# A macaron layer on one core: gate/up and down of each SwiGLU as one woven sequence, the sum of eight pairs scaled once, engines issuing in the written order

## The chip, the cores and the metric

The kernel runs on one core of one Trainium2 chip. The metric is the device time of one execution in microseconds. A core has five engines with an instruction queue each: PE multiplies matrices, ACT (ScalarE), DVE (VectorE) and POOL (GpSimd) work on tiles of 128 partitions, and SP issues the DMA transfers here. Each queue is worked off strictly in its order; semaphores make an instruction wait for another engine or a transfer, and whatever stands behind it in its queue then waits too.

## The reference, cut to what matters

One layer with 1024 tokens, 1024 features and a hidden width of 2816, all in float32. The first and the last sub-layer, both a SwiGLU with half weight, are what the change touches; the token mixers and the attention to the memory lie between.

```python
def rmsnorm(x, g):
    xf = x.astype(jnp.float32)
    y = xf * lax.rsqrt(jnp.mean(xf * xf, axis=-1, keepdims=True) + EPS)
    return (y * g.astype(jnp.float32)).astype(x.dtype)

def swiglu(h, w_gu, w_down):
    gu = h @ w_gu
    gate, up = jnp.split(gu, 2, axis=-1)
    return (jax.nn.silu(gate) * up) @ w_down
...
x = x + 0.5 * swiglu(rmsnorm(x, ffn1_norm[l]), ffn1_w_gu[l], ffn1_w_down[l])
...
x = x + mixed @ w_out[l]
x = x + memory_cross_attention(rmsnorm(x, mem_q_norm[l]), rmsnorm(mem, mem_kv_norm[l]),
                               mem_w_q[l], mem_w_kv[l], mem_w_o[l])
x = x + 0.5 * swiglu(rmsnorm(x, ffn2_norm[l]), ffn2_w_gu[l], ffn2_w_down[l])
return rmsnorm(x, final_norm)
```

## The kernel before

**Tiles.** Activations lie with features on the partitions: 8 chunks of 128 features, each for two halves of H = 512 tokens (`xT[c, hf]`, tiles `x`). The normalised chunks are kept as a rounded part and a rest (`hh`, `hl`), and every float32 product is made of three matmuls of such parts (high by high, high by low, low by high; lines L258 to L260). The inverse RMS of a token is not in the activations: it is a row `rs` by which the gate and the up sums are multiplied later.

**Strassen's scheme.** The SwiGLU products are done by a scheme with seven products for a 2x2 block product (`PRODUCTS`): A11·B11, S1·T1, S2·T2, A12·B21, S3·T3, S4·B22, A22·T4. Their sums build up in the PSUM banks X, Y and Z (two buffers of each). A `job` is one such set for 256 columns of a weight matrix: it loads the weight (tiles `r`), POOL makes the sums S (L235 S1, L238 S2, L241 S4, L244 S3), and `blocks.factor` splits each factor into `f` (high part on ACT, L342; rest on DVE, L343). A product is jn x 3 matmuls of 128x512, with jn = 4 in gate and up. After a product its bank is read while later products run, and a bank is reused by another product about three products later.

**One SwiGLU.** The 2816 hidden features are 11 pairs of chunks. For each pair there is a gate job and an up job. `weave` lays the seven products of the jobs of two streams one beside the other, the second stream LAG = 3 products behind, and `prepare` makes the factors AHEAD = 6 products early. The reads (`summed`): L615 (ACT copies X or Y to a tile E), L622 (DVE adds a bank), L632 (times `rs`, on POOL, or on DVE for one block of four), L598 and L599 (`gated`: Silu on ACT, then a second multiplication by `rs` on POOL), L643 (DVE, up times gate). `store` (L689 to L694) forms T1 to T4 of the pair and sends seven tiles to DRAM.

**Down.** When gate and up are done, a second `weave` multiplies by the down weight: feature pairs in the groups (0,4), (4,4), (8,3), each with four jobs e = 0 to 3 of two output chunks. The last group of the second SwiGLU has two pairs, and the eleventh pair is multiplied plainly at the end. `staged` brings the stored tiles back into four landing buffers `sg` (L717), ACT copies the high part (L719), DVE makes the rest (L720). `fetch` (L729) brings x back from DRAM, and each bank is then added by DVE as x += 0.5·bank (L754, seven times per job and group).

**Ends.** At the start of a SwiGLU `sums` makes the T tiles of the input (L561 to L578). After its last group, ACT squares each finished chunk (`arrive`, L160), POOL adds the squares into `sqa` (L162), PE sums them over the partitions (tile `nm`, L187), and the chunks are lifted for the mixers (`lift_chunk`, L172 on ACT, L173 on DVE). A generator (`side`) normalises the memory rows between the pairs of the first SwiGLU.

**What sets the order.** The kernel names the engine of every instruction; the place in the engine's queue is chosen by the tile scheduler, within what the data allow.

## Time and profile before

| | us |
|---|---|
| three runs | 2341.6, 2348.91, 2348.41 (median 2348.41) |
| the profiled execution | 2342.71 |
| its span, first to last instruction | 2340.7 |
| DVE busy | 1602.7 (68%) |
| ACT busy | 980.3 (42%) |
| POOL busy | 765.0 (33%) |

The first SwiGLU fills about 0 to 700 us of the span, the second about 1667 us to the end. The profile's page lists the busy time of each engine; the table by stretches of time lists for each stretch the busy time of PE, PE's weight loads (PEld), DVE, ACT and POOL with the number of instructions, then the granted clock of PE (1.00 is full), the mean busy share of the 16 DMA engines and the GB/s moved. A busy PE may be a slow PE: the number of matmuls in a stretch says more than its busy time.

### The profile page before, as it was taken

The page shows a single profiled execution, that of the slowest core. Times are in us where ns is not written, and L with a number is a line of the kernel's source. Part 1 is how long each engine was busy: PE and PEld are TensorE (multiplying, and loading weights), DVE is VectorE, ACT ScalarE, POOL GpSimd, SP SyncE. Part 2 cuts the span into 40 slices and gives each one's busy share as a digit, 9 for nine tenths or more (in the row PEclk, how much of TensorE's full clock was granted, in tenths as well). Part 3 has the DMA queues.
Part 4 walks back from the last instruction along what each step waited for, and adds up shares of the span by engine and source line. Part 5 has one row for each costly group of instructions (what it writes and reads, how often), then busy time and mean ns, then how long its engine had stood idle before and what let it go on. Part 6 is the DMA issues. An engine that isn't in the chain of part 4 may idle for free.

```text
span 2340.7 us, 31188 instructions
## 1 busy us (share of the span) xinstructions
PE 2232.2 (95%) x11314; PEld 1869.8 (80%) x11314; DVE 1602.7 (68%) x2768; ACT 980.3 (42%) x1791; POOL 765.0 (33%) x720
## 2 busy tenths in 40 slices
PE   8899999889999999999999999999979999989998
PEld 6788878777878788887978888887768888877787
DVE  6755665768774878878697546567755555586777
ACT  6433443435454635345364333234533333343444
POOL 3555555522240202011022020001356565642223
PEclk9999999999999999999999999999989999999999
DMA  6232343465331000000014411111333333255432
GB/s 221 89 110 95 130 135 110 144 215 178 120 121 38 28 28 28 28 28 28 19 46 147 124 37 54 46 37 46 124 99 110 114 103 117 91 175 191 143 104 81
DMA packets 197529, 226.98 MB, mean 97 GB/s; under 512 B 10688, under 2 KB 139776, under 8 KB 197376
## 3 DMA queue, kind: packets, MB, share of 16 engines
q1 hardware_dynamic: 197376, 225.00, 29.7%
q8 instruction: 89, 1.46, 0.3%
q14 instruction: 64, 0.52, 0.1%
HBM read 165.45 MB, written 59.51 MB: 96 GB/s over the span
## 4 chain that ended last, share of the span: by engine, by line
PE 75%; DVE 12%; ACT 4%; issue 4%; POOL 3%; DMA 2%; SPq 0%; ACTq 0%; DVEq 0%; POOLq 0%
PE X L258 8%; PE X L259 8%; PE X L260 8%; PE acc L115 4%; PE acc L117 4%; PE acc L116 4%; PE Y L258 4%; PE Y L259 4%; PE Y L260 4%; DVE om L925 2%; PE Z L260 2%; PE Z L259 2%; PE Z L258 2%; PE q L115 2%; PE q L116 2%
## 5 line engine op out<-in xcount | busy, mean ns | idle before, releaser
L343 DVE TENSOR_TENSOR f<-S,f 128x512 fp32r<-128x512 f32 (+2 forms) x256 | 211.9, 830 | 175.6 <-ACT f L342 162.5
L342 ACT ACTIVATE f<-S 128x512 fp32r<-128x512 f32 (+2 forms) x256 | 155.1, 608 | 217.4 <-PE X L260 90.7
L258 PE MATMUL X<-T,f 128*128 128x512 f32 x488 | 196.3, 402 | 38.9 <-ACT E L615 15.4
L343 DVE TENSOR_TENSOR f<-r,f 128x512 fp32r<-128x512 f32 (+2 forms) x208 | 172.7, 833 | 65.8 <-ACT f L342 65.6
L258 PE MATMUL X<-hh,f 128*128 128x512 f32 x488 | 191.4, 392 | 14.2 <-DVE x L754 6.6
L259 PE MATMUL X<-T,f 128*128 128x512 f32 x488 | 195.0, 399 | 0.0
L260 PE MATMUL X<-T,f 128*128 128x512 f32 x488 | 194.8, 399 | 0.0
L342 ACT ACTIVATE f<-r 128x512 fp32r<-128x512 f32 (+2 forms) x208 | 125.6, 610 | 159.1 <-PE X L260 90.1
L259 PE MATMUL X<-hl,f 128*128 128x512 f32 x488 | 190.1, 389 | 0.0
L260 PE MATMUL X<-hh,f 128*128 128x512 f32 x488 | 190.0, 389 | 0.0
L235 POOL TENSOR_TENSOR S<-r,r 128x512 f32<-128x512 f32 (+2 forms) x64 | 95.2, 1488 | 188.3 <-DMA r<-in_ffn_w_down_dram 117.5
L115 PE MATMUL acc<-hh,wh 128*128 128x512 f32 (+1 forms) x384 | 152.8, 398 | 0.0
L117 PE MATMUL acc<-hh,wl 128*128 128x512 f32 (+1 forms) x384 | 145.2, 378 | 0.0
L116 PE MATMUL acc<-hl,wh 128*128 128x512 f32 (+1 forms) x384 | 144.6, 377 | 0.0
L258 PEld LDWEIGHTS X<-T,f 128*128 128x128 f32 x488 | 94.9, 195 | 61.7 <-ACT E L615 16.3
L922 POOL TENSOR_SCALAR_AFFINE_SELECT om<-om 128x128 f32<-128x128 f32 x64 | 25.4, 397 | 354.0 <-ACT om L917 353.8
L241 POOL TENSOR_TENSOR S<-r,S 128x512 f32<-128x512 f32 (+2 forms) x64 | 81.6, 1275 | 165.2 <-DVE f L343 162.2
L244 POOL TENSOR_TENSOR S<-r 128x512 f32<-128x512 f32 (+2 forms) x64 | 97.3, 1520 | 107.9 <-DVE f L343 99.3
L599 POOL TENSOR_TENSOR E<-E,rs 128x512 f32<-128x512 f32 x84 | 121.1, 1443 | 31.0 <-ACT E L598 25.8
L598 ACT ACTIVATE E<-E 128x512 f32<-128x512 f32 x84 | 52.9, 631 | 186.0 <-POOL E L632 165.8
L632 POOL TENSOR_TENSOR E<-E,rs 128x512 f32<-128x512 f32 x60 | 100.6, 1677 | 89.6 <-DVE E L622 89.6
L258 PEld LDWEIGHTS X<-hh,f 128*128 128x128 f32 x488 | 91.7, 188 | 37.2 <-ACT f L342 8.2
(451 smaller groups left out, 6449.9 us busy)
## 6 DMA issues: line engine op xcount, KB each, us to landing
r<-in_ffn_w_gu_dram SPq DMA_DIRECT2D x86, 512.0 KB
r<-in_ffn_w_down_dram SPq DMA_DIRECT2D x34, 512.0 KB
wraw<-in_w_in_dram SPq DMA_DIRECT2D x20, 512.0 KB
wraw<-in_mem_w_kv_dram SPq DMA_DIRECT2D x16, 512.0 KB
T<-in_x_dram SPq DMA_DIRECT2D x8, 512.0 KB
fx<-x SPq DMA_DIRECT2D x16, 256.0 KB
x<-fx SPq DMA_DIRECT2D x16, 256.0 KB
xs<-x SPq DMA_DIRECT2D x16, 256.0 KB
```

The lines of the kernel that those rows point to most:

```text
L115: nc.tensor.matmul(ps, lh, rh, start=start, stop=False)
L116: nc.tensor.matmul(ps, lh, rl, start=False, stop=False)
L117: last_mm[0] = nc.tensor.matmul(ps, ll, rh, start=False, stop=stop).ins
L235: nc.gpsimd.tensor_tensor(src, a[1, 0], a[1, 1], op=ALU.add)
L244: nc.gpsimd.tensor_tensor(src, a[0, 0], a[1, 0], op=ALU.subtract)
L258: nc.tensor.matmul(ps, fh[:, i, :], bh, start=a, stop=False, skip_group_check=True)
L259: nc.tensor.matmul(ps, fh[:, i, :], bl, start=False, stop=False, skip_group_check=True)
L260: nc.tensor.matmul(ps, fl[:, i, :], bh, start=False, stop=z, skip_group_check=True)
L342: nc.scalar.activation(hi, src, AF.Copy)
L343: nc.vector.tensor_tensor(lo, src, hi.bitcast(F32), op=ALU.subtract)
L599: nc.gpsimd.tensor_tensor(s, s, rs[hf], op=ALU.mult)
L632: eng.tensor_tensor(out, src, rs[hf], op=ALU.mult)
```

## The change

**Issue order.** A helper, `in_order`, ties each instruction of an engine to the one issued before it, so that the instructions of both SwiGLUs stand in the queues of DVE, ACT, POOL and PE as they are written. (In the rows below and in the profile of the changed kernel they have the line of that helper, L83 or L80.) What is written is: after each product its bank's read, then deferred steps (`defer`, counted in products), then the preparation of later products. A factor is made in stages with leads of their own: weight load 7 products ahead, POOL sum 6, high part 5, rest 4; the stored tiles of down are fetched 7 ahead, and split 4 and 3 ahead.

**One sequence.** The down jobs are appended to the streams of the gate and the up jobs, so one `weave` covers both. `staged` transfers straight into the tile that later holds the rest; the landing buffers for it are gone.

**Scaled once.** For the first eight pairs the second multiplication by `rs` after the Silu is left out (`NORMED`). Down's sum over these eight pairs is collected unscaled in E tiles: in group (0,4), four of the seven reads are ACT copies and three are DVE additions; after group (4,4), `to_x` multiplies the sum by `rs` on POOL, fetches that chunk of x from DRAM, and adds half of the sum to it on DVE two products later. The sixteen fetches of x at the start of down are gone. The last group adds as before.

**Starts and ends.** The T sums of the input are written as short interleaved chains, T3 and the sending of x to DRAM after the first products; the first pair's `store` comes 14 products later. The lifts of the first SwiGLU's result are written into the sequence as the chunks come free (in rotated places), and the last square of each half is not added by POOL but summed by PE as a second operand (`apart`). The memory rows are normalised in smaller steps from pair 2 on. The number of 512-column matmuls is the same, and the stages between the SwiGLUs keep their order but for a few rows.

```diff
+    class in_order:
...
+                    with tc.issue_after(self.last):
+                        done = getattr(self.eng, name)(*args, **kw)
+                self.last = done.ins
...
+    dve, act, pl_, pe = (in_order(eng) for eng in (nc.vector, nc.scalar, nc.gpsimd, nc.tensor))
...
-    def arrive(c, hf, g0, sqp, acc, lift=True, eng=None):
+    def arrive(c, hf, g0, sqp, acc, lift=True, apart=False):
...
-        if hf in acc:
-            nc.gpsimd.tensor_tensor(acc[hf], acc[hf], sq, op=ALU.add)
+        if first or apart:
+            acc.setdefault(hf, []).append(sq)
         else:
-            acc[hf] = sq
+            nc.gpsimd.tensor_tensor(acc[hf][0], acc[hf][0], sq, op=ALU.add)
...
-    AHEAD, LAG = 6, 3
+    LAG = 3
+    LOAD, SUM, FETCH, HI, LO, FETCHED_HI, FETCHED_LO = 7, 6, 7, 5, 4, 4, 3
...
+        def stages(self, n):
+            early = n == 0
+            return ((LOAD, self.load), (SUM, self.sum), (HI - early, self.hi), (LO - early, self.lo))
...
         def run(self):
             for i, (j, n) in enumerate(self.order):
-                self.prepare(i + 1)
+                late, self.late = self.late, []
                 j.product(n)
-                self.prepare(i + 1 + AHEAD)
+                for entry in late:
+                    entry[0] -= 1
+                    if entry[0]:
+                        self.late.append(entry)
+                    else:
+                        entry[1]()
+                self.prepare(i)
...
+    NORMED = 8
...
+                    (dve if key == 21 else pl_).tensor_tensor(out, src, rs[hf], op=ALU.mult)
+
+                    def gated():
+                        done = act.activation(out, out, AF.Silu)
+                        if p >= NORMED:
+                            pl_.tensor_tensor(out, out, rs[hf], op=ALU.mult)
...
+                    pairs.defer(1, gated)
...
+            def staged(p, bk, n):
+                hi, lo = slot(blk, bk, n)
+                nc.sync.dma_start(out=lo.bitcast(F32), in_=ad[p][bk])
+                return hi, lo
...
+            def to_x(c, hf):
+                xt = xT[c, hf]
+                t = pools["sg"].tile([P, H], F32, name="sg")
+                nc.sync.dma_start(out=t, in_=xd[c, hf])
+                pl_.tensor_tensor(xt, xt, rs[hf], op=ALU.mult)
+                pairs.defer(2, lambda: dve.scalar_tensor_tensor(xt, xt, 0.5, t, op0=ALU.mult, op1=ALU.add))
...
+                        for hi, lo in Bg[bk]:
+                            if what == 1:
+                                act.activation(hi, lo.bitcast(F32), AF.Copy)
+                            else:
+                                dve.tensor_tensor(lo, lo.bitcast(F32), hi.bitcast(F32), op=ALU.subtract)
...
+                    if p0 == 0 and (fk == "A22" or not final):
+                        xT[2 * e + c, hf] = E()
+                        act.activation(xT[2 * e + c, hf], bank[to], AF.Copy)
+                        return
+                    xt = xT[2 * e + c, hf]
+                    if ends:
+                        dve.scalar_tensor_tensor(xt, bank[to], 0.5, xt, op0=ALU.mult, op1=ALU.add)
...
+                            for at in may[:1 if e == 2 else DC]:
+                                waiting.remove(at)
+                                lo = lift_chunk(*at, lift, act, dve, (at[0] + 6) % DC)
+                                pairs.defer(1, lambda lo=lo: next(lo, None))
+                    else:
+                        dve.tensor_tensor(xt, bank[to], xt, op=ALU.add)
+                        if p0 and final:
+                            to_x(2 * e + c, hf)
...
+            streams = [[gate_job(p) for p in range(1, FP)], [up_job(p) for p in range(1, FP)]]
+            for p0, pn in GROUPS[:2] + last_group:
+                get, fetch = fetches(p0, pn)
+                for e in range(4):
+                    streams[e % 2].append(down_job(p0, pn, e, get, fetch))
+            pairs = weave(*streams)
...
+            pairs.defer(1, lambda: flow([sums_4(2), sums_4(3)], 2))
+            pairs.defer(2, x_away)
+            pairs.defer(4, open_mp)
+            pairs.defer(14, lambda: store(0, s[0][0], s[1][0], s[0][1], s[1][1]))
+            pairs.run()
```

Three places show the order. First, **ACT at the start of the second SwiGLU**, before (hh and T are splits of the input's sums, f<-S splits of POOL's weight sums, f<-r splits of weights, E<-X and E<-Y reads of PSUM):

```order
L577 ACTIVATE hh4_1_15938<-t2_15816 128x512
L577 ACTIVATE hh6_1_15942<-t3_15842 128x512
L342 ACTIVATE f_15996<-S_15994 128x512
L342 ACTIVATE f_16001<-S_15999 128x512
L598 ACTIVATE E_15870<-E_15870 128x512
L598 ACTIVATE E_15871<-E_15871 128x512
L342 ACTIVATE f_16020<-S_15737 128x512
L342 ACTIVATE f_16038<-S_15999 128x512
L615 ACTIVATE E_15982<-X_15969 128x512
```

and now (t are the input's sums on their way; x0_1 is an input chunk):

```order
L83 ACTIVATE f_15862<-r0_15778 128x512
L83 ACTIVATE f_15864<-S_15782 128x512
L83 ACTIVATE f_15870<-S_15866 128x512
L83 ACTIVATE e_15886<-X_15873 128x512
L83 ACTIVATE T42_15890<-t_15725 128x512
L83 ACTIVATE T43_15892<-t_15726 128x512
L83 ACTIVATE e_15909<-Y_15896 128x512
L83 ACTIVATE t_15911<-x0_1_11763,G_83 128x512
L83 ACTIVATE t_15913<-x2_1_12681,G_83 128x512
L83 ACTIVATE hh0_1_15917<-t_15911 128x512
L83 ACTIVATE hh2_1_15920<-t_15913 128x512
```

All of the input's splits stood ahead of the first gate read E_15982<-X; now the first gate read, e_15886<-X, stands ahead of T4's and T3's, and behind other copies of S.

Second, **DVE where the first SwiGLU passes from gate/up to down**, before (T40 to T42 and the `hl` are rests of stored tiles out of the landing buffers `sg`, x0_0<-X is the first read of down):

```order
L343 TENSOR_TENSOR f_4168<-S_4107,f_4168 128x512
L343 TENSOR_TENSOR f_4205<-r1_3968,f_4205 128x512
L720 TENSOR_TENSOR T40_4187<-sg_4185,T40_4187 128x512
L720 TENSOR_TENSOR T41_4192<-sg_4190,T41_4192 128x512
L720 TENSOR_TENSOR T42_4197<-sg_4195,T42_4197 128x512
L754 SCALAR_TENSOR_TENSOR x0_0_3958<-X_3973,x0_0_3958 128x512
L343 TENSOR_TENSOR f_4222<-r1_4073,f_4222 128x512
L754 SCALAR_TENSOR_TENSOR x0_0_3958<-Z_4171,x0_0_3958 128x512
```

and now (E<-X, E<-Z and E<-Y are reads of PSUM; the rests are made in place):

```order
L83 TENSOR_TENSOR hl1_1_4040<-hl1_1_4040,hh1_1_4039 128x512
L83 TENSOR_TENSOR hl3_1_4043<-hl3_1_4043,hh3_1_4042 128x512
L83 TENSOR_TENSOR hl5_1_4046<-hl5_1_4046,hh5_1_4045 128x512
L83 TENSOR_TENSOR hl7_1_4049<-hl7_1_4049,hh7_1_4048 128x512
L83 TENSOR_TENSOR E_4006<-X_3934,E_4006 128x512
L83 TENSOR_TENSOR f_4156<-r1_3760,f_4156 128x512
L83 TENSOR_TENSOR f_4180<-r1_3954,f_4180 128x512
L83 TENSOR_TENSOR T40_4111<-T40_4111 128x512
L83 TENSOR_TENSOR T41_4113<-T41_4113 128x512
L83 TENSOR_TENSOR T42_4115<-T42_4115 128x512
L83 TENSOR_TENSOR T43_4117<-T43_4117 128x512
L83 TENSOR_TENSOR E_4063<-Y_3993,E_4063 128x512
```

Each four rests of a fetched factor are now followed by a read and two weight splits, and ahead of a read here stand at most four of them, a store's four sums and a few splits.

Third, **DVE at the end of the first SwiGLU**, before (hl<-x,G are the lifts, x<-X the last group's reads):

```order
L754 SCALAR_TENSOR_TENSOR x6_0_4371<-Z_5852,x6_0_4371 128x512
L173 SCALAR_TENSOR_TENSOR hl3_0_5726<-x3_0_4067,G_83,hh3_0_5725 128x512
L173 SCALAR_TENSOR_TENSOR hl5_0_5849<-x5_0_4242,G_83,hh5_0_5848 128x512
L173 SCALAR_TENSOR_TENSOR hl0_1_5558<-x0_1_3960,G_83,hh0_1_5557 128x512
L173 SCALAR_TENSOR_TENSOR hl2_1_5690<-x2_1_4065,G_83,hh2_1_5689 128x512
L173 SCALAR_TENSOR_TENSOR hl4_1_5819<-x4_1_4240,G_83,hh4_1_5818 128x512
L173 SCALAR_TENSOR_TENSOR hl1_1_5518<-x1_1_3964,G_83,hh1_1_5517 128x512
L173 SCALAR_TENSOR_TENSOR hl3_1_5650<-x3_1_4069,G_83,hh3_1_5649 128x512
L173 SCALAR_TENSOR_TENSOR hl5_1_5782<-x5_1_4244,G_83,hh5_1_5781 128x512
L754 SCALAR_TENSOR_TENSOR x7_1_4377<-X_5754,x7_1_4377 128x512
L173 SCALAR_TENSOR_TENSOR hl6_0_5867<-x6_0_4371,G_83,hh6_0_5866 128x512
L754 SCALAR_TENSOR_TENSOR x6_1_4373<-Y_5790,x6_1_4373 128x512
```

and now (E are the finished chunks):

```order
L83 SCALAR_TENSOR_TENSOR E_4473<-X_5693,E_4473 128x512
L83 SCALAR_TENSOR_TENSOR hl1_0_5807<-E_4387,G_83,hh1_0_5806 128x512
L83 SCALAR_TENSOR_TENSOR hl3_0_5810<-E_4552,G_83,hh3_0_5809 128x512
L83 SCALAR_TENSOR_TENSOR hl4_0_5813<-E_4423,G_83,hh4_0_5812 128x512
L83 SCALAR_TENSOR_TENSOR E_4521<-Y_5734,E_4521 128x512
L83 SCALAR_TENSOR_TENSOR hl0_1_5829<-E_4239,G_83,hh0_1_5828 128x512
L83 SCALAR_TENSOR_TENSOR hl2_1_5832<-E_4368,G_83,hh2_1_5831 128x512
L83 SCALAR_TENSOR_TENSOR E_4742<-X_5693,E_4742 128x512
L83 SCALAR_TENSOR_TENSOR hl1_1_5850<-E_4199,G_83,hh1_1_5849 128x512
L83 SCALAR_TENSOR_TENSOR hl3_1_5853<-E_4332,G_83,hh3_1_5852 128x512
L83 SCALAR_TENSOR_TENSOR hl5_1_5856<-E_4473,G_83,hh5_1_5855 128x512
L83 SCALAR_TENSOR_TENSOR hl4_1_5859<-E_4521,G_83,hh4_1_5858 128x512
```

Eight lifts stood in a row between the reads x6_0<-Z and x7_1<-X; now at most three lifts stand between two reads.

More of the change, by code (lines that the diff above doesn't have):

```diff
@@ L667, in swiglu @@
-            s = [[s0p.tile([P, H], F32, name=f"s{m}") for m in range(2)]]
-            scaled(s, 0)
-            tps = ExitStack()
-            tp = pool(tps, "tp")
-            t3 = []
-            for j in range(4):
-                t3.append(sums(j, tp))
-                for c in (2 * j, 2 * j + 1):
+                    dve.tensor_tensor(out, src, g[p][key], op=ALU.mult)
+                    if side and p >= 2:
+                        if "side" not in stack:
+                            stack["side"] = side(psx, "aux", pools["mp"])
+                        next(stack["side"], None)
@@ new lines, in swiglu @@
+            pools["e0"] = pool(st, "e0", 2)
+            s = [[pools["sg"].tile([P, H], F32, name="sg") for m in range(2)] for hf in range(2)]
+            if stored:
+                late = blk.raw.tile([P, 4, 2 * P], F32, name="r0").rearrange("p a b -> p (a b)")
+                early, late = s[0], [late[:, m * H:(m + 1) * H] for m in range(2)]
+                for hf, to in ((0, early), (1, late)):
+                    for m in range(2):
+                        nc.sync.dma_start(out=to[m], in_=gps[hf][m])
+            else:
+                early, late = gps
@@ new lines, in swiglu, with between @@
+            tps = ExitStack()
+            tp = pool(tps, "tp", 2)
+            def between():
+                for hf, src in ((0, early), (1, late)):
+                    for m in range(2):
+                        yield from scaled(s[hf][m], src[m], hf)
+                pairs.start(1)
+                yield
+                pairs.start(2)
+                yield
+                pairs.start(3)
+            flow([sums_12(j, pools["e0"].tile([P, H], F32, name="e") if j < 2 else tp.tile([P, H], F32, name="t"))
+                  for j in range(2)] + [between()]
+                 + [sums_12(j, tp.tile([P, H], F32, name="t")) for j in range(2, 4)], 3)
@@ L763, in swiglu @@
[L763 to L771 removed]
+                xp.close()
```

488 lines of the change are left out of this document (289 added, 199 removed).

## The prediction

> **What bounds the kernel now.** I read the page first, then a table by stretches of 60 us, then PE's waits, then the timeline around the long ones.
>
> ```profile
> span 2340.7 us, 31188 instructions
> ...
> PE 2232.2 (95%) x11314; PEld 1869.8 (80%) x11314; DVE 1602.7 (68%) x2768; ACT 980.3 (42%) x1791; POOL 765.0 (33%) x720
> ```
>
> PE is busy 95% of the span, so only PE's losses can be won: time without a matmul, and time at a lower clock. Where they lie shows in the number of matmuls per stretch (columns: PE, PEld, DVE, ACT, POOL busy with counts, granted clock, DMA share, GB/s).
>
> ```profile
> 60.00:120.00 60.00, 53.92 (x224) 43.34 (x222) 45.29 (x66) 26.45 (x49) 32.44 (x22) 0.94 0.27 88
> 120.00:180.00 60.00, 60.00 (x266) 49.71 (x265) 34.49 (x46) 20.77 (x36) 34.66 (x24) 1.00 0.33 106
> 180.00:240.00 60.00, 59.31 (x263) 48.77 (x262) 34.02 (x49) 24.61 (x42) 31.61 (x23) 1.00 0.31 100
> ...
> 300.00:360.00 60.00, 58.53 (x262) 47.93 (x261) 38.91 (x57) 23.09 (x43) 30.73 (x21) 1.00 0.39 128
> ...
> 420.00:480.00 60.00, 51.58 (x218) 41.89 (x218) 47.01 (x63) 29.03 (x51) 25.60 (x16) 0.94 0.56 178
> 480.00:540.00 60.00, 56.32 (x241) 45.87 (x240) 39.48 (x56) 19.56 (x33) 21.66 (x13) 0.97 0.56 192
> 540.00:600.00 60.00, 57.58 (x255) 47.40 (x254) 45.17 (x67) 25.28 (x42) 16.65 (x13) 1.00 0.47 154
> 600.00:660.00 60.00, 58.76 (x260) 48.38 (x259) 45.51 (x69) 28.83 (x49) 17.37 (x16) 1.00 0.47 147
> 660.00:720.00 60.00, 52.70 (x234) 43.41 (x234) 42.50 (x63) 28.02 (x46) 22.26 (x21) 0.94 0.26 89
> ...
> 1680.00:1740.00 60.00, 47.97 (x202) 39.21 (x201) 39.15 (x51) 26.77 (x46) 34.38 (x22) 0.89 0.28 88
> ...
> 2040.00:2100.00 60.00, 52.24 (x217) 42.38 (x216) 49.01 (x61) 28.30 (x50) 27.31 (x18) 0.91 0.54 167
> 2100.00:2160.00 60.00, 57.29 (x247) 47.02 (x246) 39.12 (x56) 20.28 (x34) 17.80 (x13) 0.97 0.54 188
> 2160.00:2220.00 60.00, 57.81 (x256) 47.57 (x255) 47.14 (x66) 26.25 (x44) 16.80 (x13) 1.00 0.49 154
> ```
>
> The stretch from 120 us is a full one: 266 matmuls in 60 us, 0.2256 us each. A matmul missing against 266 is worth that much, whatever took its place, a wait or a slow clock. So the SwiGLUs lose: at the first start (60 to 120) 42 matmuls, 9.5 us; among the pairs (180, 300) 3 + 4, 1.6 us; at the first passage from gate/up to down (420 to 540) 48 + 25, 16.5 us; between down's groups (540 to 660) 11 + 6, 3.8 us; at the second start (1680) 64, 14.4 us; at the second passage (2040 to 2160) 49 + 19, 15.3 us; between its groups (2160) 10, 2.3 us. At the first end (660 to 720) 16 of the 234 are the one-column matmuls of the norm, so 218 count: 48, 10.8 us. Together 74.2 us: no rearrangement of the SwiGLUs can win more. Who ends the waits (us in total, times, longest):
>
> ```profile
> PE X L258 <- ACT E L615: 18.7, 4, 12.0
> PE X L258 <- DVE x L754: 17.3, 7, 4.2
> PE X L258 <- DVE E L622: 12.9, 2, 6.5
> ...
> PE nm L187 <- POOL sqa L162: 3.1, 1, 3.1
> ```
>
> They are waits for a read of bank X, on ACT or DVE. The timeline shows what held the reads back:
>
> ```profile
> 470.63 0.80 PE L258 MATMUL X<-T,f 128*128 128x512 f32 x1 [6.45 <-DVE E L622]
> ```
> ```profile
> 487.83 2.97 DVE L720 TENSOR_TENSOR T<-sg,T 128x512 fp32r<-128x512 f32 x3
> 490.72 0.68 DVE L754 SCALAR_TENSOR_TENSOR x<-X,x 128x512 f32<-128x512 f32 x1
> ```
> ```profile
> 689.48 6.85 DVE L173 SCALAR_TENSOR_TENSOR hl<-x,G,hh 128x512 fp32r<-128x512 f32 x8
> 696.25 0.68 DVE L754 SCALAR_TENSOR_TENSOR x<-X,x 128x512 f32<-128x512 f32 x1
> ```
> ```profile
> 1697.09 5.25 POOL L244 TENSOR_TENSOR S<-r 128x512 f32<-128x512 f32 x1 [4.42 <-DVE T L578]
> ```
> ```profile
> 1711.44 0.63 ACT L342 ACTIVATE f<-S 128x512 fp32r<-128x512 f32 x1 [5.66 <-POOL S L238]
> 1711.98 0.58 ACT L615 ACTIVATE E<-X 128x512 f32<-128x512 f32 x1
> ```
>
> A read that PE needs stands in its queue behind work that is needed later, or that itself waits: behind three rests of stored tiles (490), behind eight lifts (689), behind a split that waits for POOL (1711). It is a matter of order, not of throughput: even in the worst stretch DVE is busy 49.01 of 60 us.
>
> The clock adds to it:
>
> ```profile
> 470.60:474.70 4.10, 4.07 (x10) 3.24 (x11) 4.10 (x7) 1.78 (x3) 0.00 (x0) 0.50 0.76 263
> ```
> ```profile
> 1712.60:1717.10 4.50, 4.49 (x11) 3.56 (x12) 1.17 (x2) 0.45 (x1) 1.28 (x1) 0.50 0.97 319
> ```
>
> After the waits of 6.45 and 12.0 us the clock is 0.50 for over 4 us, 10 or 11 matmuls where about 20 fit. Between down's groups, with 2.5 us lost from 540, it stays 1.00.
>
> [...]
>
> **The change part by part.** *Order at the two passages.* Now every product's read stands first after it, and four rests of one fetched factor stand between two reads. The work stays: over the 14 products around the passage I count 54 DVE instructions.
>
> ```profile
> L754 DVE SCALAR_TENSOR_TENSOR x<-X,x 128x512 f32<-128x512 f32 x48 | 32.9, 686 | 28.1 <-PE X L260 28.0
> ...
> L720 DVE TENSOR_TENSOR hl<-sg,hh 128x512 fp32r<-128x512 f32 x44 | 36.6, 863 | 1.4 <-ACT hh L719 1.4
> ```
>
> At 0.67 us each (45.17 us for 67 in the stretch from 540) that is 36 us, against 14 x 12 x 0.2256 = 37.9 us of PE: it fits, barely. At the 0.863 us of the rests everywhere it would be 46.6, 8.7 too long. A read may come up to three products (8.1 us) late before PE waits. I take the nearer end, since most of the 54 are splits and sums as in that stretch, and leave 2 us lost at each passage. Gain 14.5 + 13.3.
>
> *Transfers.* Without landing buffers, 28 tiles of 256 KB and four weight loads' 2 MB arrive and 1.8 MB of stores leave in those 37.9 us: 11.3 MB, 298 GB/s on average.
>
> ```profile
> 490.00:500.00 10.00, 8.55 (x30) 6.63 (x31) 6.86 (x11) 1.17 (x3) 1.29 (x1) 0.83 1.06 389
> ```
>
> With the queues full, 389 GB/s went through while the sixteen x tiles came. Those now come one by one in group (4,4). SP's queue holds the loads in order; a tile's transfer waits for the last matmul on its slot, seven products before use, and the weight load queued behind it is itself seven products early. Four tiles, 1 MB, need 2.7 us at 389 GB/s; the split on ACT follows three products (8.1 us) after the issue. I cost it at nothing; the other end is the second rival.
>
> *Scaled once.* Removed per SwiGLU: 28 of the POOL multiplications; added: 16 POOL multiplications and 16 DVE additions; four of group (0,4)'s seven reads per job, 16, go from DVE to ACT.
>
> ```profile
> L599 POOL TENSOR_TENSOR E<-E,rs 128x512 f32<-128x512 f32 x84 | 121.1, 1443 | 31.0 <-ACT E L598 25.8
> ```
>
> POOL saves 12 x 1.443 = 17.3 us per SwiGLU, under matmuls in the full stretches, where PE waits for nothing: worth nothing there. DVE saves 16 x 0.686 in the first group and pays about as much from the second group on. POOL's and DVE's added steps stand after the reads and are due only when the last group reads that chunk, a group later. I leave 2 us lost between groups in each SwiGLU (before 3.8 and 2.3): gain 1.8 + 0.3.
>
> An L754 addition, with one operand in PSUM, takes 686 ns on average; rests of two SBUF operands average 863, and one POOL sum took 5.25 us beside back-to-back DVE work. [...]
>
> *The starts.* The first gate read stood behind all of the input's splits; now T3's and T4's come after it. What remains is the chain POOL sum, split, POOL sum, split in front of the first products, which the row at 1711 shows, and POOL beside a busy DVE. If nothing remained I would gain 23.9 us, and nothing if POOL's 5.25 us strike again. Between these ends I leave 6 us lost at each, about one such long POOL sum, since the blocks of DVE work are cut up but the first products still need three sums each. Gain 3.5 + 8.4.
>
> *The first end.* Eight lifts (6.85 us) ahead of a read become three (2.2 us, under 8.1 us of slack).
>
> ```profile
> 703.87 1.26 POOL L162 TENSOR_TENSOR sqa<-sqa,sq 128x512 f32<-128x512 f32 x1 [2.04 <-ACT sq L160]
> ```
> ```profile
> 705.19 2.15 PE L187 MATMUL nm<-ones,sqa 128*128 128x1 f32 x16 [3.08 <-POOL sqa L162]
> ```
>
> POOL's 1.26 us drop out of the wait for the norm, 3.08 us, and so does the half clock after it. The norm's own 2.15 us stay, and I leave 1.4 us of wait: 3.5 lost, gain 7.3.
>
> *Memory rows* in smaller steps: gain the 1.6 us.
>
> The sum: 14.5 + 13.3 + 1.8 + 0.3 + 3.5 + 8.4 + 7.3 + 1.6 = 50.7 us. The profiled execution took 2342.71 us, 2.0 more than its span: 2342.7 - 50.7 = **2292 us**. It lies 5.7 us below the median of the three runs, near their lowest; runs that fall as those two did would give 2298, inside the range. Own range: all unknowns at their good end (nothing left at starts and passages) 2276, at twice what I leave everywhere, 23 us more, but not all at once, 2310.
>
> **The rivals.** *DVE and POOL collide in the last groups.* From group (4,4) to the last, 14 products are 7 x 2.71 + 7 x 2.03 = 33.2 us of PE in the first SwiGLU and 7 x 2.71 + 7 x 1.35 = 28.4 in the second; I count 51 and 46 DVE instructions there. At 0.82 us, between 0.67 and 0.863, they need 41.8 and 37.7: 8.6 and 9.3 too long, less the 4 counted, plus two times 1.7 for the half clock: 17 more, 2309. For it: the 863 ns row. Against it: 600 to 660 holds 69 DVE instructions in 45.51 us. 0.11.
>
> *The transfers come late.* Down's first group and each change of group then wait on ACT for tiles, with the reads behind: six places at about the 4.2 us of the longest wait for a sum, 25 us: 2317, or 2324 with the half clock. For it: 298 of 389 GB/s asked. Against it: the average leaves a quarter free. 0.11.
>
> *Slower: the written order stalls in every pair.* If a split of S waits on ACT for POOL, the next read of X stands behind it, and a scheduler no longer moves it ahead. Mechanism: the chain S1 sum, split, S2 sum, split. Slack is 8.1 us; with both sums at 5.25 us instead of 1.3 the chain takes 10.5 + 0.7 + 0.6 = 11.8, a wait of 3.7 and half clock of 1.7 after it. Over 20 turns of pairs that is 108 us: 2400. It decides from half of the turns on (54 us against my 51). Against it: in the stretch from 120, 24 POOL instructions run in 34.66 us beside DVE at 34.49 of 60, none long, and PE waits for nothing. 0.08.
>
> *It does not do what it says*: the same waits return at the same places in another order, 2342. Against it: the waits name single reads behind movable work. 0.03.
>
> **How the numbers follow.** Forecast (2276 to 2310) 0.63, better still 0.04, the two rivals on the same side 0.11 each, slower 0.08, no change 0.03. The range reaches from 2270 to the late transfers, 2326, and leaves out the last two. A difference under 0.3%, 7 us, can't be told from none. Faster 0.88, same 0.04, slower 0.08.
>
> **What would show it.** Right: 262 or more matmuls in every stretch of the two passages, no wait for E or x above 3 us, clock 1.00 from 480 on to the norm, no read behind eight lifts. Wrong: DVE over 55 of 60 us in the last groups (first rival), ACT waiting for DMA into hl or T (second), waits of one length in every pair (slower).

## The result, and the profile after

The changed kernel took 2331.05 us (median of four runs, 2328.79 to 2331.66) against 2348.29 us. The ratio is 0.9933 (95% interval 0.9921 to 0.9945): faster, but by 17 us and not by the forecast 51. The profiled execution has a span of 2329.9 us, against 2340.7 us, so 10.8 us of the gain can be placed in the two traces. Reading the start of the same instruction off both timelines gives this account:

| place | before | after | gain so far | forecast so far |
|---|---|---|---|---|
| pair 1's last tile for B sent off, first SwiGLU | 125.2 | 119.6 | 5.6 | 3.5 |
| the same of pair 9 | 435.5 | 426.3 | 9.2 | 5.1 |
| last product of the first SwiGLU | 700.3 | 685.4 | 14.9 | |
| spreading of the norm | 712.8 | 706.0 | 6.8 | 28.7 |
| first norm of the attention to the memory | 1411.0 | 1410.2 | 0.8 | 28.7 |
| last q projection | 1666.4 | 1665.0 | 1.4 | 28.7 |
| pair 1's last tile for B sent off, second SwiGLU | 1754.3 | 1746.7 | 7.6 | 37.1 |
| the same of pair 9 | 2059.0 | 2051.3 | 7.7 | 37.1 |
| first norm of the end | 2312.2 | 2301.2 | 11.0 | 50.7 |
| end of the span | 2340.7 | 2329.9 | 10.8 | 50.7 |

Up to each of these places PE has done the same matmuls in both kernels, but for the spreading: ahead of it stand eight more of the mixer's in the changed kernel, 1.8 us, so that the gain there is 8.6 us of like work. Up to the first SwiGLU's pair 9 the gain runs ahead of the forecast. Then it falls behind at three kinds of place: in down (both times), at the norm, and in a stage that the change doesn't touch. The table by stretches of the changed kernel (columns as before) shows the first:

```profile
420.00:480.00 60.00, 55.57 (x234) 44.29 (x233) 54.55 (x64) 30.71 (x58) 29.11 (x19) 0.97 0.68 229
480.00:540.00 60.00, 60.00 (x267) 49.67 (x266) 37.71 (x54) 28.90 (x54) 17.62 (x12) 1.00 0.46 142
540.00:600.00 60.00, 58.43 (x257) 47.87 (x256) 58.05 (x69) 18.55 (x34) 36.01 (x22) 1.00 0.44 134
600.00:660.00 60.00, 54.37 (x218) 42.17 (x217) 57.26 (x74) 26.88 (x53) 30.77 (x22) 0.94 0.55 177
...
2040.00:2100.00 60.00, 56.73 (x248) 45.91 (x247) 51.81 (x59) 29.75 (x56) 29.15 (x19) 1.00 0.67 229
2100.00:2160.00 60.00, 60.00 (x266) 49.67 (x265) 37.70 (x54) 30.74 (x58) 17.18 (x12) 1.00 0.46 141
2160.00:2220.00 60.00, 58.43 (x257) 47.88 (x257) 58.13 (x70) 18.09 (x34) 34.10 (x22) 1.00 0.44 136
2220.00:2280.00 60.00, 54.67 (x226) 42.40 (x225) 55.72 (x87) 21.84 (x50) 27.14 (x24) 0.97 0.34 110
```

The passages from gate/up to down (420 to 540, 2040 to 2160) now miss 32 and 18 matmuls against 266, 7.2 and 4.1 us at 0.2256 us each, where 16.5 and 15.3 us were lost. Between the groups it is the reverse: 540 to 660 misses 57 matmuls, 12.9 us (before 3.8), and 2160 to 2280 misses 49, 11.1 us (before 14 and 3.2 us). In the first stretch behind each passage (540, 2160) DVE is busy 58.05 and 58.13 us of 60, with 69 and 70 instructions, 0.84 and 0.83 us each; before it was 45.17 us for 67 and 47.14 us for 66.

PE's waits of the changed kernel say the same in total: the 12.0 us wait is gone, one of 6.0 us and many of 1 to 2.5 us are left (us in total, times, longest).

```profile
PE X L83 <- DVE E L83: 13.6, 11, 2.5
PE X L83 <- ACT e L83: 10.8, 2, 6.0
...
PE acc L136 <- DMA hl<-msl: 4.3, 1, 4.3
...
PE nm L206 <- ACT sg L181: 3.3, 1, 3.3
```

What DVE does in the stretch that loses most is in its timeline, with POOL's beside it (start, duration):

```profile
622.69 0.68 DVE L83 SCALAR_TENSOR_TENSOR E<-Y,E 128x512 f32<-128x512 f32 x1
623.29 0.54 DVE L83 TENSOR_TENSOR f<-r,f 128x384 fp32r<-128x384 f32 x1
623.76 0.68 DVE L83 TENSOR_TENSOR E<-Y,E 128x512 f32<-128x512 f32 x1
624.36 0.68 DVE L83 SCALAR_TENSOR_TENSOR E<-E,sg 128x512 f32<-128x512 f32 x1
624.96 4.62 DVE L83 TENSOR_TENSOR hl<-hl,hh 128x512 fp32r<-128x512 f32 x3
629.50 0.68 DVE L83 SCALAR_TENSOR_TENSOR E<-X,E 128x512 f32<-128x512 f32 x1
630.10 0.54 DVE L83 TENSOR_TENSOR f<-S,f 128x384 fp32r<-128x384 f32 x1
630.57 0.54 DVE L83 TENSOR_TENSOR f<-r,f 128x384 fp32r<-128x384 f32 x1
631.03 0.68 DVE L83 TENSOR_TENSOR E<-X,E 128x512 f32<-128x512 f32 x1
```
```profile
624.51 1.68 POOL L83 TENSOR_TENSOR E<-E,rs 128x512 f32<-128x512 f32 x1 [3.50 <-DVE E L83]
626.55 1.06 POOL L83 TENSOR_TENSOR S<-r,r 128x384 f32<-128x384 f32 x1 [0.36 <-DMA r<-in_ffn_w_down_dram]
627.57 1.46 POOL L83 TENSOR_TENSOR S<-r,S 128x384 f32<-128x384 f32 x1
```

E<-E,sg is the new addition of x, E<-E,rs the new multiplication. Three rests, hl, take 4.62 us while POOL is at work on the new multiplication and two sums, and 1.88 us at 639.95, with POOL idle; a read with a PSUM operand keeps its 0.68 us beside POOL (554.10, within POOL's multiplication from 553.65 to 555.34). Behind the three rests stand a read, two splits and then the read E<-X (631.03) for which PE waits 1.49 us, to 631.86. The clock then makes it dearer:

```profile
630.00:640.00 10.00, 8.51 (x25) 6.50 (x24) 10.00 (x15) 4.70 (x11) 4.47 (x3) 0.66 0.50 151
```

It is at 0.50 from 631.2 to 638.0, 6.8 us, so, counting half of the time at 0.50 as lost, here and below, 3.4 of the 10.8 us lost between 600 and 660 are the clock's. Behind a wait of 1.78 us at 2241 it is at 0.50 for another 3.4 us.

At the norm, the changed kernel's table in finer stretches shows the second loss:

```profile
686.00:688.00 2.00, 0.98 (x4) 0.45 (x3) 2.00 (x3) 0.71 (x2) 0.87 (x5) 1.00 0.47 135
688.00:690.00 2.00, 0.00 (x0) 0.00 (x0) 2.00 (x5) 2.00 (x4) 0.00 (x0) 0.80 0.36 133
690.00:692.00 2.00, 1.70 (x8) 1.70 (x9) 2.00 (x5) 1.81 (x3) 0.00 (x0) 0.50 0.35 131
...
696.00:698.00 2.00, 2.00 (x8) 1.81 (x8) 1.10 (x2) 0.00 (x0) 0.00 (x0) 0.50 0.00 0
...
700.00:702.00 2.00, 2.00 (x7) 1.52 (x6) 1.09 (x7) 0.00 (x0) 0.00 (x0) 0.50 0.97 271
702.00:704.00 2.00, 2.00 (x8) 1.60 (x7) 0.00 (x0) 0.00 (x0) 0.00 (x0) 0.78 0.70 207
```

PE still waits 3.3 us for the last square, the clock halves while it waits, and it stays halved from 689.2 to 702.8, 13.7 us. The norm's one-column matmuls, now two operands for each half, fill the time from the wait to 696.8. From the last product to the spreading it takes 20.6 us instead of 12.5; 1.8 of the 8.1 us are the eight matmuls more.

### The profile page after: what moved, and what is told of

It is laid out like the page before. It is cut to its first block, busy times and chain, and to the rows that moved or that the text cites. A ratio compares the mean times of both kernels' runs of the same rounds, so it can differ in the third digit from the quotient of the medians.

```text
span 2329.9 us, 31085 instructions
## 1 busy us (share of the span) xinstructions
PE 2240.2 (96%) x11330; PEld 1872.3 (80%) x11330; DVE 1691.9 (73%) x2770; ACT 973.8 (42%) x1823; POOL 734.6 (32%) x686
## 5 line engine op out<-in xcount | busy, mean ns | idle before, releaser
L83 PE MATMUL X<-T,f 128*128 128x512 f32 x1464 | 349.7, 394 | 15.2 <-ACT e L83 10.8
L83 PEld LDWEIGHTS X<-T,f 128*128 128x128 f32 x1464 | 277.7, 190 | 76.4 <-ACT e L83 11.7
L83 PE MATMUL X<-hh,f 128*128 128x512 f32 x975 | 316.1, 394 | 14.8 <-DVE E L83 13.2
L83 ACT ACTIVATE f<-S 128x512 fp32r<-128x512 f32 (+2 forms) x256 | 154.4, 608 | 347.5 <-POOL S L83 347.1
L83 DVE TENSOR_TENSOR f<-S,f 128x512 fp32r<-128x512 f32 (+2 forms) x256 | 257.6, 1013 | 27.2 <-ACT f L83 25.9
L83 PEld LDWEIGHTS X<-hh,f 128*128 128x128 f32 x975 | 185.1, 190 | 58.7 <-ACT f L83 8.8
L83 POOL TENSOR_TENSOR E<-E,rs 128x512 f32<-128x512 f32 x112 | 180.0, 1608 | 121.7 <-DVE E L83 100.7
L83 DVE TENSOR_TENSOR f<-r,f 128x512 fp32r<-128x512 f32 (+2 forms) x192 | 199.7, 1058 | 0.4
L83 POOL TENSOR_TENSOR S<-r,r 128x512 f32<-128x512 f32 (+2 forms) x64 | 96.7, 1512 | 314.6 <-DVE E L83 87.3
L83 PE MATMUL X<-hl,f 128*128 128x512 f32 x488 | 192.3, 394 | 2.7 <-DVE hl L83 2.7
L83 PE MATMUL Y<-T,f 128*128 128x512 f32 x732 | 177.0, 390 | 0.2 <-DVE T L83 0.2
L83 PEld LDWEIGHTS Y<-T,f 128*128 128x128 f32 x732 | 137.2, 188 | 29.6 <-DVE T L83 1.2
L83 PE MATMUL Y<-hh,f 128*128 128x512 f32 x488 | 160.6, 389 | 0.0
L83 PE MATMUL Z<-hh,f 128*128 128x512 f32 x488 | 160.6, 389 | 0.0
L83 POOL TENSOR_TENSOR S<-S,r 128x512 f32<-128x512 f32 (+2 forms) x64 | 82.3, 1286 | 213.7 <-DVE f L83 213.7
L83 ACT ACTIVATE E<-X 128x512 f32<-128x512 f32 x102 | 60.5, 593 | 192.8 <-PE X L83 192.8
L83 DVE TENSOR_TENSOR E<-X,E 128x512 f32<-128x512 f32 x98 | 67.3, 687 | 84.3 <-PE X L83 84.1
L83 DVE TENSOR_TENSOR E<-Y,E 128x512 f32<-128x512 f32 x64 | 44.0, 688 | 97.6 <-PE Y L83 97.6
```

What stands on the lines that cost most here:

```text
L83: done = getattr(self.eng, name)(*args, **kw)
```

## The experiments

The ratios are to the kernel before, which was timed beside each of them; the changed kernel's is 0.9933.

**1. Without the scaling step.**

```diff
                         dve.tensor_tensor(xt, bank[to], xt, op=ALU.add)
-                        if p0 and final:
-                            to_x(2 * e + c, hf)
```

> The changed kernel without the whole step that scales the sum of eight pairs and adds it to x (16 POOL multiplications, 16 fetches, 16 DVE additions per SwiGLU). It leaves out x itself, the half weight and one factor rs. Theory A (these steps saturate DVE, partly by holding it up through POOL): the last groups no longer lose matmuls, DVE between 560 and 660 us falls from 100% to under 85%, and the time falls by about 20 us (11 in the first SwiGLU, 9 in the second) to about 2311. Rival B (the written order or the rests made in place slow the last groups, whatever these steps do): within 4 us of 2331, DVE still full.

Measured: 2310.03 us, ratio 0.9849 (0.9833 to 0.9865). Its row for the worst stretch:

```profile
600.00:660.00 60.00, 59.22 (x262) 48.76 (x261) 56.55 (x79) 30.63 (x60) 28.83 (x23) 1.00 0.49 160
```

262 matmuls instead of 218: theory A. The stretch from pair 9 to the norm got 12.1 us shorter in the first SwiGLU, 8.7 in the second; 3.4 and 1.7 us of that are a clock that falls less. The written order and the rests made in place are still there, so rival B fails. DVE is as busy as before in this row, but with 79 instructions done, some of them of the next stage: what fell is the time per instruction (0.72 us, from 0.77) and the backlog. Under 85%, as expected, it is only from 540 to 600 (43.36 of 60 us).

**2. The multiplication on POOL back among the pairs.**

```diff
-    NORMED = 8
+    NORMED = 0
...
-                pl_.tensor_tensor(xt, xt, rs[hf], op=ALU.mult)
```

(and four multiplications for the first pair, after its product with up).

> The changed kernel with the second multiplication by rs put back on POOL for all pairs, and the POOL multiplication taken out of the scaling step; the fetch and the DVE addition of x stay. Theory A1 (POOL's multiplications hold up DVE's instructions on two tiles): 16 POOL instructions of 1.69 us fewer in the last groups, DVE there at about 0.75 us an instruction and not 0.87, most of the loss gone: 2315 to 2320, while the 28 more POOL multiplications among the pairs cost nothing. A2 (only the number of DVE instructions counts, which stays): within 4 us of 2331. If the pairs can't take the 28 multiplications, slower, with waits of one length in every pair.

Measured: 2323.16 us, ratio 0.9900 (0.9886 to 0.9915). The rows of the two group stretches:

```profile
540.00:600.00 60.00, 59.56 (x263) 49.06 (x262) 52.60 (x72) 20.84 (x38) 17.48 (x12) 1.00 0.47 148
600.00:660.00 60.00, 57.02 (x248) 45.82 (x248) 56.19 (x80) 27.50 (x53) 26.85 (x20) 1.00 0.56 179
```

DVE does 72 instructions in 52.60 us, 0.73 us each instead of 0.84, with the same work to do; only POOL's 36.01 us have become 17.48. That is A1. From pair 9 to the norms 8.3 and 6.7 us are won, 3.4 and 1.7 of them by the clock; the total is less, and short of A1's 2315 to 2320, since the first SwiGLU needs 2.3 us more up to pair 9 and a stage between the SwiGLUs 2.9. Among the pairs the multiplications cost nothing: from pair 3 to 9, where 16 of them stand, both kernels need 230.0 us, and from pair 2 to 9 of the second SwiGLU, with 20, 266.6 and 266.5. The 2.3 us arise before pair 3.

**3. The last squares added by POOL.**

```diff
-arrive(d, hf, GMIX, sqp, acc, False, (d, hf) in ((7, 0), (6, 1)))
+arrive(d, hf, GMIX, sqp, acc, False, False)
```

> The changed kernel, but POOL adds the last square of each half again, so PE sums one operand per half. Theory C (the second operand doubles the one-column matmuls, which at half clock last 6.5 us against 2.15 before): the norm's matmuls last 2 to 3.5 us, POOL adds 1.3 us of wait, sum -2 us, 2329. Rival D (PE was going to wait for the norm's chain anyway, so the doubling is hidden): +1 us, 2332.

Measured: 2332.11 us, ratio 0.9942 (0.9928 to 0.9957), no difference to the changed kernel. In the trace the norm's matmuls are as short as theory C has it, after a longer wait:

```profile
692.74 3.58 PE L206 MATMUL nm<-ones,sqa 128*128 128x1 f32 x16 [4.24 <-POOL sqa L185]
```

From pair 9 to the spreading of the norm it is 2.7 us shorter (277.0 against 279.8 us), with the clock at 0.50 for 10.2 us instead of 13.7, which is 1.7 of the 2.7. From there to the attention 5.1 us are lost again, as much as 17.1 us at 0.50 instead of 6.8 cost. C holds at its place, and nothing of it reaches the end, which is D's time.

**4. Fewer preparations ahead of the first product.**

```diff
-            pairs.start(to=2)
+            pairs.start(to=0)
```

> The changed kernel, but only the preparations due before the first product stand ahead of it, not those of two products more (two splits of weights and two of sums, on ACT ahead of the first gate read). Theory E (the first gate read is late by its place in ACT's queue): the wait of 4.8 and of 6.0 us at the two starts shrink by about 1 to 2 us each, with the half clock after them 3 to 6 us in all, 2326 to 2328. Rival F (the read waits for its tile, which T4's sums hold, or later products now wait for their factors): no gain, or up to 4 us slower.

Measured: 2344.32 us, ratio 0.9985 (0.9976 to 0.9995). PE's waits:

```profile
PE X L83 <- DVE f L83: 11.1, 2, 6.0
PE X L83 <- ACT e L83: 7.7, 2, 4.4
```

The read's waits shrink from 10.8 to 7.7 us as E says, and two new waits, for factors that are now late, cost 11.1 us: F on balance, and dearer than the 4 us that it allowed.

**5. The memory's loads ahead of x's**, in the stage between the SwiGLUs (SP's order; `mem_last` is the last of the memory's loads):

```diff
-        nc.sync.dma_start(out=xT[c, hf], in_=xs[c, hf])
+        with tc.issue_after(mem_last[0]):
+            nc.sync.dma_start(out=xT[c, hf], in_=xs[c, hf])
```

> The changed kernel, but in the stage between the SwiGLUs the sixteen loads of x are put behind the eight loads of the normalised memory in SP's queue. Theory G (the 4.3 us that PE waits for a memory tile near 1240 us, and the half clock after it, come from x loads queued ahead of it, which wait for POOL): the wait goes, the stage from the first load of the memory's weights to the attention falls from 246 to about 240 us, 2326. Rival H (the tiles into which the memory is loaded come free no earlier, or the transfers are bound by DMA): wait and time stay, or x then comes late for the output projection and it gets slower.

SP's queue of the changed kernel shows what it was to undo, six loads of x ahead of the last loads of the memory, and PE's wait after them:

```profile
1225.70 11.14 SPq L1436 DMA_DIRECT2D x<-xs  x6
1236.93 0.86 SPq L1401 DMA_DIRECT2D hh<-msh  x2
1237.84 0.90 SPq L1401 DMA_DIRECT2D hl<-msl  x2
```
```profile
1245.31 0.39 PE L136 MATMUL acc<-hl,wh 128*128 128x256 f32 x1 [4.32 <-DMA hl<-msl]
```

Measured: 2327.41 us, ratio 0.9910 (0.9895 to 0.9925), an interval that just overlaps the changed kernel's. The wait for hl is gone from the trace, but the stage is only 1.6 us shorter (244.7 us, 240.1 in the kernel before), and the stage after it 1.5 longer. The clock takes part of it back: it is at 0.50 for 6.8 us in the stage instead of 3.4, and for 3.4 us in the next instead of none, 1.7 us each. G names the wait rightly and not the whole loss.

**6. x added in the second halves of the groups.** On top of experiment 2, the additions are called at the first read of e = 2 of each of the first two groups, one per product:

```diff
+                    if (e, fk) == (2, "A11") and not ends:
+                        for n in range(8):
+                            at = (4 * (p0 > 0) + n // 2, n % 2)
+                            pairs.defer(1 + n, lambda at=at: to_x(*at))
...
-                        if p0 and final:
-                            to_x(2 * e + c, hf)
```

(a chunk that has x is then added to with half weight).

> As the kernel without POOL's scaling, and the 16 additions of x are moved out of the products in which a new group's tiles are split: eight into the second half of group (0,4), eight into the second half of (4,4), one per product. The number of instructions is the same on every engine. Theory A (too much DVE work in the first half of a group): the last groups come near the kernel without the step, about 8 us better than the 2323 of its predecessor: 2314 to 2317. Rival A3 (the total of DVE work counts, not its place): within 2 us of 2323.

Measured: 2310.99 us, ratio 0.9843 (0.9824 to 0.9863).

```profile
600.00:660.00 60.00, 58.86 (x260) 48.21 (x259) 55.95 (x79) 29.92 (x58) 28.07 (x23) 1.00 0.50 159
```

260 matmuls where experiment 2 has 248, with the same instructions. From pair 9 to the norms it needs 247.8 and 240.9 us, 3.3 and 2.3 less than experiment 2 (1.7 of the 3.3 by the clock), and what experiment 1 needs without any such step (247.3 and 241.2). Theory A over A3: place counts. (The fetches of x move with their additions.) The median is 12 us lower, more than these 5.6; of the rest, 6.1 us lie in the stage with the memory's loads, which the edit doesn't touch. There the clock is at 0.50 for 3.4 us, in experiment 2 for 13.7, which accounts for 5.1 of the 6.1.

**7 and 8. Together.** Experiment 7 is 5 and 6, experiment 8 adds 3.

> Both of the two before together: the sum of their gains if they are independent, about 2309 to 2312 where both theories hold.

> The kernel before it, and POOL adds the last squares again. In the earlier run of that part the stretch from the last pair to the norm was 2.6 us shorter, but the middle stage 6.3 us longer through the later memory load. If that is so, with the memory loads first the 2.6 us remain: 2 to 3 us under the kernel before it; if the doubling of the norm's matmuls is hidden, no difference.

Measured: 2311.06 us (ratio 0.9843, 0.9828 to 0.9858) and 2309.17 us (0.9833, 0.9819 to 0.9848). Neither differs from experiment 6: the gain of 5 does not add, and that of 3 is too small to tell.

**9. The scheduler's order.** The helper no longer ties instructions:

```diff
-                if self.last is None:
+                if True:
```

> The changed kernel, but the instructions are not tied to the order in which they are written: the scheduler places them, as before the change. One sequence, stages with leads, the sum scaled once and the rest stay. Theory J (the written order is what takes the waits out of the passages): waits of 4 us and more on bank X at the two passages from gate/up to down are back, and 8 us or more are lost against 2331. Rival K (the single sequence with its early fetches does it): the passages stay as they are, within 4 us of 2331 or better.

Measured: 2345.45 us, ratio 0.9985 (0.9975 to 0.9994), by the ratios 12 us slower than the changed kernel. Where:

```profile
420.00:480.00 60.00, 54.77 (x232) 44.74 (x231) 50.85 (x66) 31.19 (x57) 27.67 (x18) 0.94 0.61 202
480.00:540.00 60.00, 59.40 (x262) 48.84 (x262) 37.72 (x51) 29.25 (x52) 16.67 (x13) 1.00 0.46 150
...
600.00:660.00 60.00, 50.27 (x203) 40.66 (x202) 54.55 (x73) 25.82 (x46) 28.52 (x21) 0.91 0.53 172
...
2040.00:2100.00 60.00, 53.66 (x229) 43.96 (x228) 47.69 (x59) 29.75 (x53) 28.10 (x19) 0.94 0.58 197
```
```profile
PE X L80 <- DVE E L80: 34.6, 12, 6.3
```

The first passage misses 38 matmuls (32 in the changed kernel, 73 before), the second 37 (18, and 68 before). J's waits are back: PE waits 5.2 us for a read at 458.5 and 6.3 us at 2084.1, and 12 us are lost. Still, 35 of the 41 matmuls won at the first passage and 31 of the 50 at the second are won without the ties, which is nearer to K. What wins them isn't separated: the single sequence with its leads, the four reads of seven that ACT took over, and the fetches of x that are gone all stay in this run.

The order pays at three places. Pair 1 of the first SwiGLU is 6.0 us later without it. From pair 9 to the last product of the first SwiGLU 3.3 us are lost, to the norm of the second 8.0; all of the 3.3 and 6.8 of the 8.0 are the clock's, which is at 0.50 for 17.1 us in each, against 10.2 and 3.4. The second start is 4.5 us better in the scheduler's order (77.2 us from the q projection to pair 1, against 81.7).

**10. Splits ahead of T4 at the starts**, on top of experiment 8:

```diff
+            pairs.start(to=2)
             flow([sums_4(0), sums_4(1)], 2)
...
-            pairs.start(to=2)
```

> The best kernel so far (2309), but at each start the splits of the first weights and sums are written ahead of T4's sums, so that ACT makes them in the 3.7 us in which it now waits for DVE, and the first gate read follows T4's splits directly. Theory L (the place in ACT's queue makes the read late): the waits of 4.8 and 6.3 us shrink by about 2 us each, 2303 to 2306 with the half clock. Rival M (DVE makes the rests of those splits first, so T4's sums and the tile that the read needs come later): no change, or 2 to 4 us slower.

Measured: 2308.33 us, ratio 0.9828 (0.9811 to 0.9844). The wait is where it was:

```profile
PE X L83 <- ACT e L83: 11.1, 2, 6.3
```

M holds, by its own reason:

```profile
71.76 1.40 DVE L83 SCALAR_TENSOR_TENSOR e<-x,G,e 128x512 f32<-128x512 f32 x2
73.98 0.60 ACT L83 ACTIVATE e<-X 128x512 f32<-128x512 f32 x1 [0.15 <-DVE T L83]
```

DVE now makes three rests of those splits first and begins T4's sums at 71.76, where the changed kernel has 70.28; ACT's read then waits for the rest of T4. The splits cost the read about 1.5 us at either place. The read's tile comes from a pool of two which the two sums for T4 hold, which fits this last wait. A tile of its own for the read wasn't tried.

**11. The last lifts behind the last read**, on top of experiment 8:

```diff
-                                lo = lift_chunk(*at, lift, act, dve, (at[0] + 6) % DC)
-                                pairs.defer(1, lambda lo=lo: next(lo, None))
+                                pairs.defer(3, lambda at=at: raise_(at))
```

(`raise_` holds the two lines taken out).

> The best kernel so far (2309), but the lifts at the end of the first SwiGLU are written three products later, so that the last ten stand behind the last read. Theory N (reads and squares are late behind lifts, and PE's 4.2 us of wait for the norm come from that): the wait falls to 1.5 to 2.5 us, under what is followed by half clock, and the time from the last product to the spreading of the norm falls from 17.6 to about 13 us: 2305. Rival O (the lifts are needed by the mixer's first matmuls at once): PE waits for them instead, no gain or 2 us slower.

Measured: 2314.06 us, ratio 0.9851 (0.9834 to 0.9868), if anything slower. The last read is now prompt, and the last square is not:

```profile
678.53 0.69 DVE L83 SCALAR_TENSOR_TENSOR E<-X,E 128x512 f32<-128x512 f32 x1 [0.25 <-PE X L83]
...
681.34 1.06 ACT L115 ACTIVATE wh<-wraw 128x1024 fp32r<-128x1024 f32 x1 [2.33 <-DMA wraw<-in_w_in_dram]
682.31 0.61 ACT L181 ACTIVATE sg<-E 128x512 f32<-128x512 f32 x1
```

Between the read (678.53) and its square (682.31) ACT stands at a split of the mixer's weights, which the scheduler put there and which waits for its transfer. N fails: with the lifts away the wait is 4.3 us, as in experiment 8 (4.2). O has the time about right and not the reason: a wait of 3.0 us for DVE is new in the mixer, at 703.7, but DVE had done its last lift at 689.3 and stood idle for 7.1 us in between. Where that wait comes from stays open.

**The best version** is that of experiment 6 (2310.99 us; 10 adds 8's parts and the start, 2308.33, with overlapping intervals): about 1.6% under the kernel before, where the change as made gave 0.7%.

## Why the prediction was right or wrong

- *The bound and the waits.* Right. PE's losses in the SwiGLUs moved as reads moved in their queues.
- *The two passages.* Half right in mechanism, and short in size: 7.2 and 4.1 us stay lost where I left 2 each. DVE needs 54.55 of 60 us in the first, which "it fits, barely" should have priced higher. I put the whole gain down to the order; experiment 9 keeps 35 of 41 and 31 of 50 matmuls without it, by the single sequence or the reads and fetches taken off the passages.
- *Transfers.* Right: no wait of PE or ACT for a staged tile's transfer shows in down (410 to 660, 2035 to 2290), with 229 GB/s in the passages.
- *Scaled once.* This is the step that failed. It had the added POOL and DVE steps "due only when the last group reads that chunk, a group later", and left 2 us between groups. Measured are 12.9 and 11.1 us: 20 of the 40 us by which the traces fall short of the forecast; 7.3 are missing at the passages, the rest mainly at the first end and between the SwiGLUs. Due later is not free: in a written order the steps stand ahead of the next rests and reads, in the products in which DVE has most to do. The first rival had this at 17 us in all, and experiment 1 measured 21; its sign, DVE over 55 of 60 us in the last groups, is in all four rows (58.05, 57.26, 58.13, 55.72). Experiment 2 puts 8.3 + 6.7 us on POOL's multiplications, experiment 6 another 3.3 + 2.3 us on the place of DVE's additions. The rival got 0.11, because I read 69 instructions in 45.51 us as room, without asking how much POOL would work beside them. After 540 us it went from 16.65 to 36.01 us. (POOL loses 32 multiplications per SwiGLU, with the first pair's four, and not 28; that doesn't touch the sum.)
- *The starts.* Nearly right in sum: 5.6 and 6.2 us gained, 3.5 and 8.4 forecast. The near match is luck in part, one being better and the other worse than forecast. What is left is one wait each of 4.8 and 6.0 us, with a different cause: the read's place behind T4's sums and the first splits (experiments 4 and 10), not POOL's sums.
- *The first end.* Right on the lifts: the wait of 4.2 us behind eight of them (697) is gone. Wrong on the norm. Its wait was to shrink to 1.4 us and the half clock to vanish. It is 3.3 us, for the last square in place of POOL's sum, and the norm's matmuls and the half clock last longer: 6.3 us of like work lost from the last product to the spreading. Experiment 3 wins 2.7 us of it back without the second operand, 1.7 by the clock.
- *Between the SwiGLUs.* Not in the sum, and wrong by that: 5.4 us lost from the spreading to the last q projection, 7.2 of like work; 6.2 of them lie in the stage with the memory's loads. The scheduler places that part anew with every edit, and it queued one more load of x ahead of the memory's. Experiment 5 shows the 4.3 us wait to come from there; of the stage only 1.6 us return, since 1.7 more go to the clock and about 1 us stays open.
- *Memory rows.* Right and mis-sized: 3.6 us for 1.6. The second SwiGLU, which has none, takes 304.6 us from pair 1 to 9 in both kernels.

On DVE beside POOL: the three rests of 4.62 us (624.96), two tiles in SBUF each, stand against 1.88 us for three without POOL (639.95); a read from PSUM took 0.68 us beside POOL (554.10) as without it (638.28). Experiment 2 agrees: with POOL's work in the stretch from 540 down from 36.01 to 17.48 us, a DVE instruction there takes 0.73 us instead of 0.84. E<-E,sg (624.36), begun just ahead of POOL's multiplication (624.51), took 0.68 us with two SBUF inputs. By what mechanism POOL lengthens the rests, the runs don't show.

On the clock: my sum let the short waits that I left cost only themselves, and theory N of experiment 11 took waits of 1.5 to 2.5 us to be under what half clock follows. No run shows such a bound. Before the change already, a wait of 2.71 us at 2110 went with 3.4 us at 0.50. In the changed kernel waits of 1.49 (631), 1.78 (2241), 2.45 (449) and 3.33 us (690) went with 6.8, 3.4, 3.4 and 13.7 us at 0.50, while none went with waits of 1.57 (570) and 2.07 us (621). The 1.7 us that my rivals added for a half clock is half of 3.4 us, which is what the waits of 3.68 and 4.22 us before the change (491, 697) went with; those of 3.1 to 4.3 us at the norm went with 3.4 to 13.7 us. In down the clock takes 6.8 us in this way, 5.1 of them between the groups, which my sum had at nothing.

## What to carry to other kernels

Before moving work to "where there is time", count each engine's instructions product by product at the new place, and price those of VectorE with two SBUF operands by what GpSimd does beside them (4.62 us for three rests here, and 1.88 us with GpSimd idle); a share of 76% over 60 us (600 to 660 before the change) hid 20 us at 93% (620 to 640). A step that is due late still has a place in the written order (another one won 3.3 and 2.3 us in experiment 6): put it into the products with the least work, one at a time. Price a short wait with the clock that may go with it (3.4 us of half clock here with one of 1.78 us). And where a scheduler places the rest of the program, expect a few microseconds of change in stages that were not touched (240 to 253 us here in the stage with the memory's loads, most of it by 0 to 17 us at half clock), and measure the stages apart.

## What the runs showed of the hardware

In the traces before and after the change every stretch at half clock lasts 3.4, 6.8, 10.2 or 13.7 us, but for the last one, which the end of the kernel cuts off. At the norm, behind waits that were much alike, 3.1 to 4.3 us, it was 3.4 us before the change (from 706.8), 6.8 in experiment 11 (685.0), 10.2 in experiment 3 (691.3) and 13.7 in the changed kernel (689.2). In each of the four, 512-column matmuls fill the last 3.4 us of it, but for at most half a microsecond; from 692.6 to 696.0 in the changed kernel the norm's one-column matmuls ran without a break, and the clock stayed at 0.50. Sixteen of these took 2.15 us before the change, at full clock but for the last half microsecond, and 3.58 us in experiment 3, where the clock had halved before they ran. In the changed kernel a 512-column matmul began every 0.43 us at 0.50 (697.3 to 702.4) and every 0.23 us at 1.00 (from 703.1).
